# Two-block network on one core: who loads in the untaken overflow branch, and which engine subtracts at the start of the second block's mixers

## The chip, the cores and the metric

The kernel runs on one core of one Trainium2 chip. The metric is the device time of one execution in microseconds (us). Before the change three runs gave 1249.91, 1245.6 and 1245.42 us; their median is 1245.6.

## What is computed

The reference chains two blocks over 256 positions of 1024 channels, all in float32. The first block has two SwiGLU layers around two attention mixers, with 16 meta tokens ahead of the sequence. The second block has two layers, each of three mixers and a mixture of 32 experts:

```
def hybrid_layer(x, ...):
    hn = rms_norm(x, norm1_g)
    proj = jnp.einsum('bsd,df->bsf', hn, w_in)
    ya = mla_mixer(...)                 # low-rank attention, 8 heads
    yb = stick_breaking_mixer(...)      # 4 heads
    yc = pool_mixer(...)                # means over windows of 2, 4, 8, 16
    x = x + jnp.einsum('bsm,md->bsd', jnp.concatenate([ya, yb, yc], axis=-1), w_out)
    return x + hier_moe(rms_norm(x, norm2_g), w_group, b_group, w_expert, b_expert,
                        w_gate, w_up, w_down)

def second_block(x, ...):
    for l in range(2):
        x = hybrid_layer(x, ...)
    return rms_norm(x, final_g)
```

`rms_norm` multiplies each position by r = rsqrt(mean(x*x) + eps) and then by a gain for each channel. In `hier_moe` a position picks one of four groups of eight experts by the largest group probability, and in it the two likeliest experts.

## The kernel before

**Weights.** All weights are one array of units of 128 x 2048 float32 (1 MB, some shorter). `Stream.load` (L308) issues one unit as a DMA on SyncE's queue into a ring of eight raw buffers. `Stream.split` cuts a unit into two tiles of 1024 columns and makes of each a pair whl: a high part, by a ScalarE cast to fp32r (L326), and a low part, raw minus high, by a subtraction (L327). VectorE subtracts, or GpSimd while `st.spare` is set. There are four whl buffers. `take` hands a tile to the matmuls; `done` frees tiles and, unless `hold` is on, makes the next splits; `release` makes the splits that were held back. A product of two split operands is three matmuls (high x high, high x low, low x high). If the next unit belongs to the experts, which use raw units unsplit, `split` only counts it in `owed`, and `restart` makes these splits once the experts are through. A split has a higher priority in the scheduler, by 60 places, unless it is called with late=False.

**Order.** The program is written once; a scheduler orders each engine's instructions, by readiness and priority. Each engine then works through its own list. The DMAs of SyncE's queue use eight semaphores in turn, so at most eight loads are on their way.

**Block 2.** For each of two layers, called layer 1 and layer 2 here: `mixers2` (565 to 663 us and 899 to 1004 us of the trace), then `moe`. `mixers2` transposes x (xT), multiplies by the gain and splits into xnh (ScalarE) and xnl (VectorE) in eight steps of `gsplit`, and takes r by `rstd`: squares sq on ScalarE (L1134), their sum ss, and three short steps rs, rs, r on VectorE (L456 to L458). The products use x times gain without r; r is multiplied in afterwards. `m2_low_products` computes four products "low" of 24 matmuls each (t = 0 to 3, `wcol2`), one whl tile each. To multiply by r along the columns, r is spread: dg = ident * r on VectorE (L1214), rb = one x dg on TensorE, a copy to SBUF on VectorE (L1216); low * rb (L1225) then frees the PSUM banks that the next products, qk, are waiting for.

In layer 1 the first splits for the mixers come from the second SwiGLU layer of block 1, whose last act is the addition of its result py to x (L1084), four VectorE instructions.

**Experts.** `moe` works in eight batches b of four experts, 12 units each (eight for gate and up, gu; four for down, y). The raw ring is lent nine more buffers there, 17 in all. The result y of a batch is split into yh (ScalarE, L435) and yl (VectorE, L436) and added into a sum by the matmuls sc.

**Overflow.** An expert has 32 slots per batch. If more positions want one, `overflow` (L1721ff.) computes the rest in a second pass, behind batch 5. It reads a flag into a register on the engines (L1725, TENSOR_LOAD) and stands in a branch (L1728). With these inputs the flag is zero and the branch is not taken, but each engine has the branch's instructions in its list and jumps over them. In the branch SyncE loads weights into the buffers of yh and yl (L1740).

Of the kernel before, what the change touches and what calls it, by code (L numbers as in the profile page):

```python
# [12 lines left out]
OP = mybir.AluOpType  # L13
# [252 lines left out]
def run(*gens):  # L266
    for g in gens:
        for _ in g:
            pass


class Stream:
# [63 lines left out]
        for i in range(s.S):  # L336
            s.split(False)

    def restart(s):

        n, s.owed = s.owed, 0
        for i in range(n):
            s.split()

    def take(s, a=None):
        while s.used not in s.tiles:
# [38 lines left out]
class KB:  # L385
    R, S = 8, 4
    E = 5
    NW = 11

    def __init__(s, es, tc, a, out, dbg=None, stop=None):  # L390
        s.es, s.tc, s.nc, s.a, s.out, s.dbg, s.stop = es, tc, tc.nc, a, out, dbg or {}, stop
# [746 lines left out]
    def mixers2(s, l, p):  # L1138
        nc, st = s.nc, s.st
        v = s.v = {}  # L1140
# [10 lines left out]
        r = v["r"] = p.tile([128, 2], F32, name="r")  # L1151
# [3 lines left out]
            s.tr(pt[k][:, i * 128:i * 128 + 128], s.x[:, i, k * 128:k * 128 + 128])  # L1155
        for k in range(8):
            s.gsplit(xh[:, k, :], xl[:, k, :], pt[k][:, :T], g[:, k:k + 1])
        s.rstd(p, r)
        v["rb"] = p.tile([128, T], F32, name="rb")
        v["mix"] = p.tile([128, 2, 256], F32, name="mix")  # L1160
        v["ph"] = p.tile([128, 2, T], F32R, name="ph")
# [40 lines left out]
    def m2_low_products(s, p):  # L1202
        st, v = s.st, s.v
        q = [s.ps("low") for t in range(4)]
        for t in range(4):
            run(s.wcol2(q[t][:, :T]))
            if t == 1:
                st.spare = True
                st.release()
                st.spare = False  # L1210
                rb = s.ps("rb", tag="y")
                for i in range(2):
                    dg = s.w(p, "dg")
                    s.nc.vector.tensor_scalar(dg[:, :128], s.ident, v["r"][:, i:i + 1], None, op0=OP.mult)  # L1214
                    s.mm(rb[:, i * 128:i * 128 + 128], s.one, dg[:, :128], i == 0, True)
                s.nc.vector.tensor_copy(v["rb"], rb[:, :T])  # L1216
        return q

# [412 lines left out]
    def experts(s, l, p, px, OH, OHT, comb):  # L1631
        nc, st = s.nc, s.st
        v = nc.vector
# [4 lines left out]
        n = 0  # L1638
# [39 lines left out]
        for b in range(NB):  # L1678
# [3 lines left out]
            for k in range(8):  # L1682
                w = unit()
# [28 lines left out]
        s.exp_set()  # L1712
        down(NB - 1, hT)
        es.close()
        st.spare = True
        st.restart()
        st.spare = False
        if l:
            s.final()

    def overflow(s, l, p):

        nc, a = s.nc, s.a
        v = nc.vector
        some = nc.values_load(s.flag[0:1, 0:1], min_val=0, max_val=1)  # L1725
        gain = s.g("n2")[:, 8 * l:8 * l + 8]
        units = a["weights"][s.moe_base[l]:s.moe_base[l] + 12 * NB].rearrange("(b n) p (e f) -> b n p e f", b=NB, e=4)
        with s.tc.If(some > 0):  # L1728
            with s.phase(f"ov{l}") as po:

                W = po.tile([128, 2, 32], F32, name="oW")
                v.tensor_scalar(W, s.place, float(SL), None, op0=OP.is_gt)
                v.tensor_mul(W, W, s.r.to_broadcast([128, 2, 32]))
                W4 = W.rearrange("p i (g e) -> p i g e", g=4)
                for i in range(2):
                    v.tensor_mul(W4[:, i], W4[:, i], s.ci[:, i, None, 0:8].to_broadcast([128, 4, 8]))

                def load(b, n, j):
                    w = p.tile([128, 512], F32, name="yh" if n % 2 else "yl")
                    nc.sync.dma_start(w, units[b, n, :, j, :])  # L1740
                    return w

                XT = p.tile([128, 8, 128], F32, name="XT", bufs=3)
                for i in range(2):
                    for k in range(8):
                        q = s.ps("ogat")
                        s.tr(q[:, :128], s.x[:, i, k * 128:k * 128 + 128])
                        nc.scalar.activation(XT[:, k, :], q[:, :128], AF.Copy, scale=gain[:, k:k + 1])
                    for e in range(32):
                        b, j = divmod(e, 4)  # L1750
                        q = s.ps("ogu")
                        for k in range(8):
                            s.mm(q, XT[:, k, :], load(b, k, j), k == 0, k == 7)
                        sg = po.tile([128, 256], F32, name="osg")
                        nc.scalar.activation(sg, q[:, :256], AF.Silu, scale=s.r[:, i])
                        hid = po.tile([128, 256], F32, name="ohid")
                        v.scalar_tensor_tensor(hid, q[:, 256:], W[:, i, e:e + 1], sg, op0=OP.mult, op1=OP.mult)
                        q = s.ps("ohT")
                        for f in range(2):
                            s.tr(q[:, f * 128:f * 128 + 128], hid[:, f * 128:f * 128 + 128])  # L1760
                        hT = po.tile([128, 256], F32, name="ohT")
                        nc.scalar.copy(hT, q[:, :256])
                        for c in range(2):
                            q = s.ps("oy")
                            for f in range(2):
                                s.mm(q, hT[:, f * 128:f * 128 + 128], load(b, 8 + 2 * c + f, j), f == 0, f == 1)
                            xs = s.x[:, i, c * 512:c * 512 + 512]
                            v.tensor_add(xs, q, xs)
# [49 lines left out]
```

## Time and profile before

| what | us |
|---|---|
| median of three runs | 1245.6 |
| profiled execution | 1246.45 |
| its span in the trace | 1244.7 |
| TensorE busy | 1110.2 (89%) |
| VectorE busy | 560.6 (45%) |
| ScalarE busy | 464.1 (37%) |
| GpSimd busy | 146.0 (12%) |

In the rows below, PE is TensorE, DVE VectorE, ACT ScalarE, POOL GpSimd and SP SyncE; SPq is SyncE's queue. Times are us from the start of the span. A row of the timeline is start, busy us, engine, line, operation, names out<-in, shape, count, and in brackets the idle time of the engine just before, with the instruction whose end ended it. A high share of busy time is a mean over stages with different limits, so each stage is to be read by itself: by what its engines wait for and by how fast its loads run.

### The profile page before, as it was taken

The page shows a single profiled execution, that of the slowest core. Times are in us where ns is not written, and L with a number is a line of the kernel's source. Part 1 is how long each engine was busy: PE and PEld are TensorE (multiplying, and loading weights), DVE is VectorE, ACT ScalarE, POOL GpSimd, SP SyncE. Part 2 cuts the span into 40 slices and gives each one's busy share as a digit, 9 for nine tenths or more (in the row PEclk, how much of TensorE's full clock was granted, in tenths as well). Part 3 has the DMA queues.
Part 4 walks back from the last instruction along what each step waited for, and adds up shares of the span by engine and source line. Part 5 has one row for each costly group of instructions (what it writes and reads, how often), then busy time and mean ns, then how long its engine had stood idle before and what let it go on. Part 6 is the DMA issues. An engine that isn't in the chain of part 4 may idle for free. (4 is left out here: it accounts for less than half of the span.)

```text
span 1244.7 us, 18667 instructions
## 1 busy us (share of the span) xinstructions
PE 1110.2 (89%) x7530; PEld 840.1 (67%) x7530; DVE 560.6 (45%) x1081; ACT 464.1 (37%) x888; POOL 146.0 (12%) x151
## 2 busy tenths in 40 slices
PE   7999999999999999998998997863889989968545
PEld 7999999888799999997997532310289864313111
DVE  5555555679857555555755111100276452101002
ACT  6444444467545444445752010000257420000002
POOL 0222221000012212225110000000033000000001
PEclk9999999999999999998999899886989998988679
DMA  9754454643214545444427999999964299999986
GB/s 364 279 182 163 154 191 175 159 182 125 80 69 172 200 172 200 173 184 143 160 102 293 387 420 420 420 417 371 420 259 158 83 363 398 420 419 419 416 359 248
DMA packets 46470, 321.20 MB, mean 258 GB/s; under 512 B 5560, under 2 KB 5688, under 8 KB 8992
## 3 DMA queue, kind: packets, MB, share of 16 engines
q1 hardware_dynamic: 44640, 314.96, 64.8%
q0 software_dynamic: 1264, 4.26, 1.6%
q8 instruction: 64, 1.05, 0.3%
q10 hardware_dynamic: 464, 0.63, 0.1%
q14 instruction: 38, 0.31, 0.1%
HBM read 317.13 MB, written 2.69 MB: 257 GB/s over the span
## 5 line engine op out<-in xcount | busy, mean ns | idle before, releaser
L326 ACT CAST whl<-raw 128x1024 fp32r<-128x1024 f32 (+1 forms) x213 | 221.1, 1040 | 258.8 <-PE pu L410 53.1
L327 DVE TENSOR_TENSOR whl<-raw,whl 128x1024 fp32r<-128x1024 f32 (+1 forms) x203 | 249.8, 1232 | 147.1 <-ACT whl L326 147.0
L410 PE MATMUL gu<-raw,XT 128*32 128x512 f32 x1024 | 141.1, 651 | 33.4 <-DMA raw<-in_weights_dram 15.7
L410 PE MATMUL pg<-xh,whl 128*128 128x272 f32 (+1 forms) x704 | 137.4, 287 | 1.0 <-DVE gt L616 1.0
L410 PE MATMUL pu<-xh,whl 128*128 128x272 f32 (+1 forms) x704 | 136.2, 284 | 0.0
L410 PEld LDWEIGHTS pg<-xh,whl 128*128 128x128 f32 x704 | 113.2, 190 | 2.2 <-issue 1.1
L410 PEld LDWEIGHTS pu<-xh,whl 128*128 128x128 f32 x704 | 112.3, 188 | 0.0
L410 PEld LDWEIGHTS gu<-raw,XT 128*32 128x32 f32 x1024 | 28.4, 115 | 108.1 <-issue 72.6
L410 PE MATMUL pg<-xl,whl 128*128 128x272 f32 (+1 forms) x352 | 100.7, 286 | 0.0
L410 PE MATMUL y<-raw,hT 128*32 128x512 f32 x512 | 84.4, 679 | 18.2 <-DMA raw<-in_weights_dram 18.2
L410 PE MATMUL pu<-xl,whl 128*128 128x272 f32 (+1 forms) x352 | 100.3, 285 | 0.0
L436 DVE TENSOR_TENSOR yl<-y,yh 128x512 fp32r<-128x512 f32 x32 | 22.1, 691 | 144.6 <-ACT yh L435 144.6
L1699 DVE SCALAR_TENSOR_TENSOR hid<-gu,comb,sg 128x256 f32<-128x256 f32 x16 | 7.7, 484 | 152.7 <-ACT sg L1697 152.7
L436 POOL TENSOR_TENSOR hl<-hid,hh 128x272 fp32r<-128x272 f32 (+1 forms) x44 | 57.7, 1312 | 123.7 <-ACT hh L435 123.7
L435 ACT CAST yh<-y 128x512 fp32r<-128x512 f32 x32 | 18.8, 586 | 142.4 <-PE y L410 104.7
L410 PEld LDWEIGHTS pg<-xl,whl 128*128 128x128 f32 x352 | 66.9, 190 | 0.8
L410 PE MATMUL sc<-yh,OHT 128*128 128x512 f32 x64 | 25.8, 487 | 45.9 <-ACT yh L435 45.9
L410 PE MATMUL pd<-hh,whl 128*128 128x272 f32 x352 | 66.7, 289 | 0.0
L410 PE MATMUL gat<-OH,x 128*128 128x256 f32 x256 | 63.9, 401 | 3.0 <-DVE OH L1582 3.0
L410 PEld LDWEIGHTS pu<-xl,whl 128*128 128x128 f32 x352 | 66.2, 188 | 0.0
L410 PEld LDWEIGHTS sc<-yh,OHT 128*128 128x128 f32 x64 | 10.5, 207 | 78.4 <-ACT yh L435 77.5
L410 PEld LDWEIGHTS gat<-OH,x 128*128 128x128 f32 x256 | 48.8, 198 | 21.4 <-issue 11.7
(410 smaller groups left out, 2038.7 us busy)
## 6 DMA issues: line engine op xcount, KB each, us to landing
raw<-in_weights_dram SPq DMA_DIRECT2D x292, 1024.0 KB, 14.2
raw<-in_weights_dram SPq DMA_DIRECT2D x4, 768.0 KB, 4.2
raw<-in_weights_dram SPq DMA_DIRECT2D x5, 512.0 KB, 7.5
dl<-line POOLq DMA_DIRECT2D x1, 1600.0 KB, 36.9
tb<-dl POOLq DMA_DIRECT2D x1, 1088.0 KB, 6.4
x<-in_x_dram SPq DMA_DIRECT2D x4, 256.0 KB, 5.0
c<-in_consts_dram POOLq DMA_DIRECT2D x1, 954.0 KB, 6.5
sm<-in_smalls_dram SPq DMA_DIRECT2D x1, 712.0 KB, 18.6
```

What stands on the lines that cost most here:

```text
L326: s.kb.nc.scalar.copy(h[:, :n], raw)
L327: (s.kb.nc.gpsimd if s.spare is True or s.spare and j else s.kb.nc.vector).tensor_sub(l[:, :n], raw, h[:, :n].bitcast(F32))
L410: s.nc.tensor.matmul(out, l, r, start=start, stop=stop, skip_group_check=True)
L435: s.nc.scalar.copy(h, x)
L436: (s.nc.gpsimd if gpsimd else s.nc.vector).tensor_sub(l, x, h.bitcast(F32))
L1699: v.scalar_tensor_tensor(hid, q[:, 256:], comb[:, b, 0:1], sg, op0=OP.mult, op1=OP.mult)
```

## The change

Five edits, all in block 2.

1. `overflow`: the flag is read on four engines only, without SyncE, and without the check of its bounds. The loads in the branch are issued by GpSimd.
2. `restart(n)` makes up to n of the owed splits, without the raised priority. It is called in `mixers2` after the fourth `gsplit` (one split), after the last (two), and after `rstd` (the rest), and no longer at the end of `moe`, where GpSimd did the subtractions.
3. The `release` in `m2_low_products` at t = 1 does its subtractions on VectorE.
4. dg is computed behind t = 0.
5. rb and its copy move from t = 1 to t = 2.

```
-    def restart(s):
-        n, s.owed = s.owed, 0
+    def restart(s, n):
+        n = min(n, s.owed)
+        s.owed -= n
         for i in range(n):
-            s.split()
+            s.split(False)
...
+    OV = (mybir.EngineType.PE, mybir.EngineType.Activation, mybir.EngineType.DVE, mybir.EngineType.Pool)
...
             s.gsplit(xh[:, k, :], xl[:, k, :], pt[k][:, :T], g[:, k:k + 1])
+            if k == 3:
+                st.restart(1)
+        st.restart(2)
         s.rstd(p, r)
+        st.restart(st.S)
...
             run(s.wcol2(q[t][:, :T]))
+            if t == 0:
+                dg = [s.w(p, "dg") for i in range(2)]
+                for i in range(2):
+                    s.nc.vector.tensor_scalar(dg[i][:, :128], s.ident, v["r"][:, i:i + 1], None, op0=OP.mult)
             if t == 1:
-                st.spare = True
                 st.release()
-                st.spare = False
+            if t == 2:
                 rb = s.ps("rb", tag="y")
                 for i in range(2):
-                    dg = s.w(p, "dg")
-                    s.nc.vector.tensor_scalar(dg[:, :128], s.ident, v["r"][:, i:i + 1], None, op0=OP.mult)
-                    s.mm(rb[:, i * 128:i * 128 + 128], s.one, dg[:, :128], i == 0, True)
+                    s.mm(rb[:, i * 128:i * 128 + 128], s.one, dg[i][:, :128], i == 0, True)
                 s.nc.vector.tensor_copy(v["rb"], rb[:, :T])
...
         es.close()
-        st.spare = True
-        st.restart()
-        st.spare = False
...
-        some = nc.values_load(s.flag[0:1, 0:1], min_val=0, max_val=1)
+        some = nc.values_load(s.flag[0:1, 0:1], engines=s.OV, min_val=0, max_val=1, skip_runtime_bounds_check_because="the flag is the result of a comparison")
...
-                    nc.sync.dma_start(w, units[b, n, :, j, :])
+                    nc.gpsimd.dma_start(w, units[b, n, :, j, :])
```

SyncE's list before, from the last loads of the first branch to the second check. The second of the two jumps behind the branch waits for all eight semaphores of SyncE's DMAs.

```order
L1740 DMA yh<-in_weights_dram 128x512
L1728 UNCONDITIONAL_BRANCH x2
L1725 ISA x2
L308 DMA raw<-in_weights_dram 128x2048 x18
L308 DMA raw<-in_weights_dram 128x1024
L308 DMA raw<-in_weights_dram 128x2048 x89
L1725 TENSOR_LOAD flag
L1728 COMPARE_AND_BRANCH
```

The same stretch of SyncE's list after.

```order
L308 DMA raw<-in_weights_dram 128x1024
L308 DMA raw<-in_weights_dram 128x2048 x74
L1732 UNCONDITIONAL_BRANCH
L308 DMA raw<-in_weights_dram 128x2048 x33
L308 DMA raw<-in_weights_dram 128x1024
L308 DMA raw<-in_weights_dram 128x2048 x74
L1732 UNCONDITIONAL_BRANCH
L308 DMA raw<-in_weights_dram 128x2048 x26
```

Of the check a plain jump without a semaphore is left on SyncE; the flag, the conditional branch, the branch's loads and the two ISA instructions, which add to the eight semaphores, have gone from its list. The first yh and yl behind the check wait for the semaphores of the queue that holds the branch's loads: SyncE's before, GpSimd's after.

VectorE before, at the start of layer 1's mixers (ss, rs, rs and r are the steps to 1/rms).

```order
L620 TENSOR_TENSOR hid<-pu,rT 128x256
L1084 SCALAR_TENSOR_TENSOR x<-py,x 128x512 x4
L441 SCALAR_TENSOR_TENSOR xnl<-xT,sm,xnh 128x256 x8
L1135 TENSOR_TENSOR ss<-ss 128x2
L456 SCALAR_TENSOR_TENSOR rs_6247<-ss,rs_6246 128x2
L457 SCALAR_TENSOR_TENSOR rs_6247<-rs_6247,rs_6246 128x2
L458 SCALAR_TENSOR_TENSOR r<-rs_6247,rs_6246 128x2
L1214 TENSOR_SCALAR dg<-ident,r 128x128 x2
L1216 COPY rb<-rb 128x256
```

VectorE after, at the same place.

```order
L622 TENSOR_TENSOR hid<-pu,rT 128x256
L327 TENSOR_TENSOR whl<-raw,whl 128x1024
L1086 SCALAR_TENSOR_TENSOR x<-py,x 128x512 x4
L327 TENSOR_TENSOR whl<-raw,whl 128x1024
L443 SCALAR_TENSOR_TENSOR xnl<-xT,sm,xnh 128x256 x8
L1137 TENSOR_TENSOR ss<-ss 128x2
L327 TENSOR_TENSOR whl<-raw,whl 128x1024
L458 SCALAR_TENSOR_TENSOR rs_6247<-ss,rs_6246 128x2
L459 SCALAR_TENSOR_TENSOR rs_6247<-rs_6247,rs_6246 128x2
L460 SCALAR_TENSOR_TENSOR r<-rs_6247,rs_6246 128x2
L1216 TENSOR_SCALAR dg<-ident,r 128x128 x2
L327 TENSOR_TENSOR whl<-raw,whl 128x1024
```

Four subtractions that stood in GpSimd's list now stand among these: one ahead of the additions to x, one ahead of xnl, one ahead of rs and one behind dg.

VectorE after, at the start of layer 2's mixers; before, xnl stands there as one row of eight, and no subtraction ahead of dg.

```order
L1673 TENSOR_TENSOR x<-sc,x 128x512 x2
L443 SCALAR_TENSOR_TENSOR xnl<-xT,sm,xnh 128x256 x4
L327 TENSOR_TENSOR whl<-raw,whl 128x1024
L443 SCALAR_TENSOR_TENSOR xnl<-xT,sm,xnh 128x256 x4
L327 TENSOR_TENSOR whl<-raw,whl 128x1024 x2
L1137 TENSOR_TENSOR ss<-ss 128x2
L327 TENSOR_TENSOR whl<-raw,whl 128x1024 x2
L458 SCALAR_TENSOR_TENSOR rs_11737<-ss,rs_11736 128x2
L327 TENSOR_TENSOR whl<-raw,whl 128x1024
L459 SCALAR_TENSOR_TENSOR rs_11737<-rs_11737,rs_11736 128x2
L460 SCALAR_TENSOR_TENSOR r<-rs_11737,rs_11736 128x2
```

Six subtractions stand ahead of r there. On TensorE rb stands behind 72 of the 96 matmuls of low in layer 1 (55 before) and behind 79 in layer 2 (48 before).

## Rows read from the trace of the kernel before

**Rows 1.** The page, 40 equal slices: TensorE busy, granted clock (tenths), GB/s.

```profile
PE   7999999999999999998998997863889989968545
PEclk9999999999999999998999899886989998988679
GB/s 364 279 182 163 154 191 175 159 182 125 80 69 172 200 172 200 173 184 143 160 102 293 387 420 420 420 417 371 420 259 158 83 363 398 420 419 419 416 359 248
```

**Rows 2.** Windows of 5 us: busy per engine, granted clock, DMA share, GB/s.

```profile
860.00:865.00 5.00, 1.94 (x6) 0.70 (x10) 0.69 (x1) 0.59 (x1) 0.00 (x0) 0.50 0.43 129
...
1195.00:1200.00 5.00, 0.71 (x2) 0.50 (x2) 0.69 (x1) 0.59 (x1) 0.00 (x0) 0.50 0.23 93
1200.00:1205.00 5.00, 5.00 (x20) 0.91 (x18) 0.00 (x0) 0.00 (x0) 0.00 (x0) 0.50 0.96 359
```

**Rows 3.** Timeline of ScalarE at the two checks.

```profile
862.43 0.59 ACT L435 CAST yh<-y 128x512 fp32r<-128x512 f32 x1 [20.86 <-SPq L1728]
...
1198.66 0.59 ACT L435 CAST yh<-y 128x512 fp32r<-128x512 f32 x1 [16.80 <-SPq L1728]
```

**Rows 4.** Waits of SyncE's queue, 840 to 920 us: total, times, longest.

```profile
SPq L1728 <- SPq L1728: 18.9, 7, 5.1
```

**Rows 5.** Timeline of TensorE around the checks.

```profile
863.06 1.22 PE L410 MATMUL sc<-yh,OHT 128*128 128x512 f32 x2 [13.55 <-ACT yh L435]
...
1171.52 3.42 PE L410 MATMUL gu<-raw,XT 128*32 128x512 f32 x16 [11.40 <-issue]
...
1183.52 1.02 PE L410 MATMUL y<-raw,hT 128*32 128x512 f32 x2 [0.49 <-DMA raw<-in_weights_dram]
```

**Rows 6.** Timeline of TensorE, start of layer 1's mixers.

```profile
567.44 0.38 PE L410 MATMUL low<-xnh,whl 128*128 128x256 f32 x1 [0.16 <-DVE xnl L441]
...
578.31 1.19 PE L410 MATMUL rb<-dg,one 128*128 128x128 f32 x4 [4.12 <-DVE dg L1214]
...
586.27 0.28 PE L410 MATMUL qk<-xnh,whl 128*128 128x256 f32 x1
```

**Rows 7.** Timeline of VectorE, start of layer 1's mixers.

```profile
563.98 2.48 DVE L1084 SCALAR_TENSOR_TENSOR x<-py,x 128x512 f32<-128x512 f32 x4 [4.19 <-PE py L410]
566.90 3.23 DVE L441 SCALAR_TENSOR_TENSOR xnl<-xT,sm,xnh 128x256 fp32r<-128x256 f32 x8 [0.44 <-ACT xnh L440]
...
575.31 2.27 DVE L457 SCALAR_TENSOR_TENSOR rs<-rs,rs 128x2 f32<-128x2 f32 x1
577.61 0.16 DVE L458 SCALAR_TENSOR_TENSOR r<-rs,rs 128x2 f32<-128x2 f32 x1
```

**Rows 8.** Timeline of GpSimd in both layers of block 2.

```profile
562.59 4.73 POOL L327 TENSOR_TENSOR whl<-raw,whl 128x1024 fp32r<-128x1024 f32 x2
...
572.88 4.67 POOL L327 TENSOR_TENSOR whl<-raw,whl 128x1024 fp32r<-128x1024 f32 x2 [2.16 <-ACT whl L326]
...
695.89 0.67 POOL L1144 TENSOR_TENSOR wr<-sm 128x288 f32<-128x288 f32 x1 [67.38 <-PE ohT L418]
...
904.36 9.37 POOL L327 TENSOR_TENSOR whl<-raw,whl 128x1024 fp32r<-128x1024 f32 x4 [207.70 <-ACT whl L326]
```

**Rows 9.** Window of 4 us behind rb in layer 1, columns as in Rows 2.

```profile
578.00:582.00 4.00, 3.69 (x17) 3.73 (x18) 1.54 (x5) 0.75 (x2) 0.73 (x1) 0.50 0.72 262
```

**Rows 10.** Timeline of TensorE, start of layer 2's mixers.

```profile
904.33 0.58 PE L410 MATMUL low<-xnh,whl 128*128 128x256 f32 x1 [4.59 <-ACT whl L326]
...
906.76 0.79 PE L410 MATMUL low<-xnh,whl 128*128 128x256 f32 x2 [1.63 <-POOL whl L327]
...
920.76 0.28 PE L410 MATMUL qk<-xnh,whl 128*128 128x256 f32 x1
```

**Rows 11.** The page's costliest groups: busy, mean ns of one, idle before.

```profile
L327 DVE TENSOR_TENSOR whl<-raw,whl 128x1024 fp32r<-128x1024 f32 (+1 forms) x203 | 249.8, 1232 | 147.1 <-ACT whl L326 147.0
```

**Rows 12.** Timeline of ScalarE, start of layer 2's mixers.

```profile
897.86 3.04 ACT L440 ACTIVATE xnh<-xT,sm 128x256 fp32r<-128x256 f32 x8 [1.55 <-PE sc L410]
```

**Rows 13.** The chain of waits, its shares of the span by line.

```profile
by line: DMA raw<-in_weights_dram 1.5%; PE y L410 0.5%; PE sc L410 0.5%; ACT sq L1778 0.2%; ACT yh L435 0.2%; DVE x L1666 0.1%; DVE raw L1792 0.1%; issue 0.1%; DVEq L1814 0.1%; DVE rs L457 0.0%; DVE rs L458 0.0%; ACT rs L448 0.0%; DVE rs L4
```

## Prediction

> **What bounds the kernel now.** I began with the page's slices [rows 1]. In the two expert stages (slices 23 to 29 and 34 to 39) the loads run at 417 to 420 GB/s, with one dip in each, 371 in slice 28 and 359 in slice 39, where TensorE is busy only 3 and 4 tenths. Outside the dips these stages last as long as their loads. In the mixers ahead of them (slices 19 to 21 and 30 to 32) TensorE is busy 8 tenths and more and the loads run far below what they reach later: there TensorE's chain is the bound. So a microsecond saved at the start of a mixer stage, or in a dip, should reach the end: what follows is TensorE's chain, and then a stream of loads whose buffers come free when the mixers are done.
>
> Next the windows of 5 us at the dips [rows 2]. In the first, 129 GB/s; against 418, the level of the stage, that is 5 x (1 - 129/418) = 3.5 us without loads. At the second, 93 and then 359 GB/s: 5 x (1 - 93/418) + 5 x (1 - 359/418) = 3.9 + 0.7 = 4.6 us.
>
> Then who waits there. ScalarE's first cast yh behind the overflow's check comes after 20.86 us of idle time in layer 1 and 16.80 in layer 2, and the releaser is SyncE's branch at L1728 [rows 3]; SyncE's queue waits at its own L1728, 18.9 us in all around the first dip [rows 4]. I read this so: SyncE gets past the branch not taken only when all its loads in flight have landed, and issues nothing meanwhile, so that the loads run dry. TensorE waits for that yh, 13.55 us in layer 1; in layer 2 it had been waiting for a load at 1183.52, just ahead of its own wait for yh [rows 5].
>
> Last the mixers' starts. In layer 1 TensorE runs 55 of the 96 matmuls of the low products from 567.44 on and then waits 4.12 us for dg up to 578.31, so from 574.19, because rb stands there [rows 6]. dg is late because r is: its second last step took 2.27 us on VectorE, the last one, of the same shape, 0.16 [rows 7]. GpSimd's two subtractions from 572.88 to 577.55 lie over the slow one and not over the fast one [rows 8]. Behind the wait TensorE's granted clock is 0.50, its 1.2 GHz level [rows 9]. In layer 2 TensorE waits 4.59 us for a cast and 1.63 more for GpSimd's first subtraction [rows 10]; GpSimd's four take 9.37/4 = 2.34 us each [rows 8], VectorE's 1.23 on average [rows 11].
>
> **The change, part by part.**
>
> 1. The check in layer 1. SyncE's branch has no wait any more, so its loads go on: 3.5 us. This holds if TensorE doesn't keep the buffers instead. Its own jump over the overflow's code stays (11.40 us in layer 2), but TensorE had made that good by 1183.52 [rows 5]. Bounds: 2 (part of the gap comes back, since each load still waits for a buffer) to 4.5 (the gap of layer 2).
>
> 2. The check in layer 2, in the same way: 4.6 us. Bounds 2.5 to 6; the upper end is for TensorE's pile of work at half clock behind the wait, whose only sign in the loads is the 0.7 us above, taken three times.
>
> 3. The mixers of layer 1. The subtractions leave GpSimd, so r is early, and rb stands 17 matmuls later: no wait for dg. At the pace of the first 55 (6.75/55, about 0.12 us each) 96 matmuls take 11.5 us, with rb's 0.6 12.1; they took from 567.44 to 586.27, where qk starts, 18.8 [rows 6]. So 6.7 us can go, 4.1 of wait and 2.6 of half clock. But VectorE's first subtraction now stands ahead of the residual additions. GpSimd still runs one from 562.59 to 564.97 [rows 8]; VectorE's would end about 1.1 behind it (an estimate, a little under its mean of 1.23), at 566.05, and the additions, now from 563.98 [rows 7], start 2.1 later. The second subtraction, 1.23 less the gap of 0.44 that stood ahead of xnl [rows 7], adds 0.8. The low products begin 2.9 later, at 570.3, and end at 582.4: 3.9 us gained. Bounds: 1.5 (TensorE's clock falls in the longer wait ahead of them; a product of 24 matmuls at 0.21 us, about their pace in layer 2 behind 906.76, instead of 0.12 costs 2.2) to 6.7 (the subtractions delay nothing).
>
> The 2.1 us rest on the row of 2.27 [rows 7]: a VectorE instruction on operands in SBUF ends when GpSimd's does. The Trainium skill, "SBUF — State Buffer", section "Who interferes with whom", has this as a rule: when a VectorE instruction with two SBUF inputs and a GpSimd one that reads SBUF meet, the later to start is blocked to the end of the other. By it the term is 3.9, and the trace agrees (2.27 against 0.16); without it the subtraction would end 1.23 behind its cast and the term would be 5.2.
>
> 4. The mixers of layer 2. All subtractions go to VectorE and the casts move up among the gain products. The first cast now stands behind the eight xnh, which begin at 897.86 and take 3.04 [rows 12], and the squares, and ends just ahead of 904.33 [rows 10]; behind the fourth xnh it starts at about 899.4 and ends at 900.4, and the subtraction ends near 901.7, against TensorE's starts at 904.33 and 906.76 [rows 10]. The first product still at half clock, 24 x 0.21 = 5.1, ends at 906.8; at 0.12 the second ends at 909.7, the third at 912.6. r's chain stands behind the sixth tile's subtraction, which waits for the second product: 909.7 + 1.05 + 1.23 = 912.0, then two steps and dg, 0.9 together: 912.9. rb stands 79 matmuls in, at 913.4, so TensorE hardly waits; qk starts at 916.1 instead of 920.76: 4.6 us. Bounds 2.5 (r two microseconds later) to 6.
>
> GpSimd's queue now holds the loads of the overflow that aren't run. It comes to the check early: L1144, the first thing behind the check in its queue, ran at 695.89 [rows 8], 150 us before anyone needs the check.
>
> **Sum:** 3.5 + 4.6 + 3.9 + 4.6 = 16.6 us. The profiled execution took 1246.45 (span 1244.7 and 1.75 around it), 0.85 above the median of 1245.6. So 1229.85 for it, and **1229.0** at the median.
>
> **The rivals.**
>
> A. The forecast, 1229.0.
>
> B. The subtractions cost VectorE's path what they cost GpSimd's: layer 1 gains 1.5, layer 2 one. For: r's chain stands behind two more subtractions, and the additions behind one. Against: each takes half of GpSimd's time. 1245.6 - 8.1 - 2.5 = 1235.0.
>
> C. The last batch runs at half clock. Now TensorE has work piled up behind the wait and keeps its clock at 9 tenths in slice 40; without the pile it works from load to load to the end. In the chain of waits its y and sc have 0.5% each [rows 13], 12.4 us of 1244.7 together; less some 3 ahead of the last load that the chain goes through, 9.4, and twice that at half clock: 1229.0 + 9.4 = 1238.4. Against: in the other expert slices, where it works from load to load, the clock is mostly 8 or 9 tenths [rows 1].
>
> D. Both delays of parts 3 and 4 are hidden: 6.7 + 5.5 + 3.5 + 5 = 20.7, 1224.9.
>
> E. Slower: GpSimd behind the check. VectorE and ScalarE now wait, at their first yl and yh, for semaphores that GpSimd sets behind its jump over some 780 rows. In layer 1 yh is due when TensorE's y is done, 863.06 less the 13.55 of wait: 849.5. The free buffers (17 less the eight on their way, at 2.5 us for a load of 1 MB) cover about 22 us of lateness; from there on each microsecond counts in full, in each layer. 40 us late would give 1245.6 - 8.5 + 2 x 18 = 1273.1. Against: GpSimd passes 150 us earlier, and TensorE's jump over as much code took 11.40 us. The Trainium skill, "Runtime: NRT & Kernel Launch", section "Instruction fetch mechanics", says that a taken branch out of the fetched window waits for its target to be fetched; it gives no price, and by TensorE's row GpSimd is still early.
>
> F. The change doesn't do what it says, and the loads still run dry. The order shows no wait at SyncE's branch. Only 8.5 us of the mixers: 1237.1.
>
> **How the numbers follow.** Chances: A 0.55, B 0.18, C 0.08, D 0.13, E 0.02, F 0.04. Half a per cent, 6.2 us, is about what a measurement of this kernel can tell from no change; faster is below 1239.4. A and D lie there whole, B and F nearly, C for the most part: 0.91; same 0.06, slower 0.03. The lower bounds sum to 8.5, the upper to 23.2: 1237.1 and 1222.4. All at one end is unlikely; C lies just outside. The range 1221.5 to 1238 leaves out E and the outer parts of B, C and F.
>
> **What would show it.** Right: no window under 400 GB/s at the two checks and no wait of ScalarE on the branch; in layer 1 no wait of TensorE ahead of rb, and from the first low product to qk about 12 us instead of 18.8; in layer 2 the first low product 2 to 3 us earlier behind the last sc, and qk 4 to 5. Wrong: low products of layer 1 over 3 us later, or at half clock (B); granted clock 0.50 behind the last load (C); ScalarE or VectorE released by GpSimd at the check (E); loads still running dry there (F).

## The result, and the profile after

The changed kernel takes 1232.51 us (median of four runs, 1226.56 to 1236.81), the kernel before 1246.42 (four runs, 1245.42 to 1249.91): ratio 0.9878, interval 0.9838 to 0.9917, wholly below 1. The forecast was 1229.0 in a range of 1221.5 to 1238. The profiled execution, 1236.81 us with a span of 1235.0, is the slowest of the four.

The page of the changed kernel, slices as in [rows 1]:

```profile
PE   7999999999999999999999998767799989978565
PEclk9999999999889999999999899778899988988687
GB/s 365 277 185 169 154 175 192 145 184 120 103 35 161 181 185 190 180 196 156 193 77 229 390 421 420 420 419 418 421 345 145 86 331 399 420 420 420 416 418 241
```

Both dips in the loads are gone: 416 to 421 from slice 24 to 29 and from 35 to 39. But PEclk has two 8s in slices 11 and 12, in the first block, where [rows 1] has 9s and where the change has no instruction. The windows of 10 us there, first of the changed kernel (busy time of PE, PEld, DVE, ACT, POOL; granted clock; DMA share; GB/s):

```profile
330.00:340.00 10.00, 10.00 (x36) 6.66 (x36) 5.37 (x23) 3.88 (x14) 0.00 (x0) 0.64 0.00 1
340.00:350.00 10.00, 10.00 (x44) 7.68 (x44) 5.43 (x22) 3.48 (x12) 0.00 (x0) 0.68 0.00 1
```

and of the kernel before:

```profile
330.00:340.00 10.00, 10.00 (x55) 7.16 (x56) 8.02 (x36) 5.64 (x21) 0.00 (x0) 1.00 0.00 1
340.00:350.00 10.00, 10.00 (x67) 8.53 (x66) 6.82 (x23) 5.07 (x17) 0.00 (x0) 1.00 0.01 2
```

In 20 us the changed kernel does 80 matmuls where the other does 122, and the first block ends 6.3 us later. A difference of 10 us in the spans thus hides one of 16 behind it. So I compare stages, each from one matmul's start to another's. The third column is a second profile of the same changed kernel.

| stage, us | before | after | after, again | forecast gain |
|---|---|---|---|---|
| to the last py (first block) | 564.5 | 570.8 | 566.7 | 0 |
| last py to first gu (mixers, layer 1) | 121.7 | 117.1 | 117.4 | 3.9 |
| first gu to last sc (experts, layer 1) | 211.3 | 208.2 | 207.8 | 3.5 |
| last sc to first gu (mixers, layer 2) | 123.5 | 119.4 | 120.3 | 4.6 |
| first gu to the last load's landing | 210.6 | 206.9 | 205.7 | 4.6 |
| last landing to the end | 13.1 | 12.6 | 12.7 | 0 |
| span | 1244.7 | 1235.0 | 1230.6 | 16.6 |

Without the first block the two profiles give 15.9 and 16.3 us, against the forecast's 16.6.

At the checks ScalarE's first yh is released by TensorE's y, 4.1 and 1.2 us after the work before it; before, it was released by SyncE's branch, after 20.86 and 16.80 [rows 3]. Timeline of ScalarE after:

```profile
848.40 0.59 ACT L437 CAST yh<-y 128x512 fp32r<-128x512 f32 x1 [4.09 <-PE y L412]
...
1179.16 0.59 ACT L437 CAST yh<-y 128x512 fp32r<-128x512 f32 x1 [1.24 <-PE y L412]
```

SyncE's queue waited 18.9 us at the branch around the first check [rows 4]. After, it has no wait at its jump there; what it waits for most, from 830 to 920 us, is an earlier load (total, times, longest):

```profile
SPq L308 <- DMA raw<-in_weights_dram: 55.4, 26, 3.0
```

Start of layer 1's mixers after: TensorE,

```profile
573.00 2.56 PE L420 MATMUL xT<-ident,x 128*128 128x128 f32 x16 [1.86 <-DVE x L1086]
576.32 0.38 PE L412 MATMUL low<-xnh,whl 128*128 128x256 f32 x1 [0.76 <-DVE xnl L443]
584.90 0.61 PE L412 MATMUL rb<-dg,one 128*128 128x128 f32 x4
588.17 0.28 PE L412 MATMUL qk<-xnh,whl 128*128 128x256 f32 x1
```

VectorE,

```profile
569.81 2.53 DVE L327 TENSOR_TENSOR whl<-raw,whl 128x1024 fp32r<-128x1024 f32 x1 [3.75 <-ACT whl L326]
572.26 2.47 DVE L1086 SCALAR_TENSOR_TENSOR x<-py,x 128x512 f32<-128x512 f32 x4
...
582.50 0.16 DVE L459 SCALAR_TENSOR_TENSOR rs<-rs,rs 128x2 f32<-128x2 f32 x1
```

and GpSimd.

```profile
568.86 2.40 POOL L327 TENSOR_TENSOR whl<-raw,whl 128x1024 fp32r<-128x1024 f32 x1
...
708.51 0.67 POOL L1146 TENSOR_TENSOR wr<-sm 128x288 f32<-128x288 f32 x1 [78.12 <-remote]
```

All times here are 6.3 later than in [rows 6 to 8] by the first block. The price that the prediction named is there: VectorE's subtraction begins at 569.81 under GpSimd's, which ends at 571.26, and ends 1.08 later; it takes 2.53 instead of 1.23, the additions start 2.0 late (572.26 less 6.27 is 565.99 against 563.98), and TensorE waits 1.86 for them ahead of xT. The step rs that took 2.27 [rows 7] takes 0.16, TensorE has no wait at rb, and from the first low product to qk there are 11.85 us instead of 18.83.

Start of layer 2's mixers after, TensorE:

```profile
899.04 0.39 PE L412 MATMUL low<-xnh,whl 128*128 128x256 f32 x1 [0.68 <-ACT whl L326]
900.30 0.50 PE L412 MATMUL low<-xnh,whl 128*128 128x256 f32 x2 [0.76 <-DVE whl L327]
910.14 0.68 PE L412 MATMUL rb<-dg,one 128*128 128x128 f32 x4 [0.35 <-DVE dg L1216]
912.70 0.28 PE L412 MATMUL qk<-xnh,whl 128*128 128x256 f32 x1
```

The waits of 4.59 and 1.63 [rows 10] have become 0.68 and 0.76, and r's chain is just not quite in time (0.35).

### The profile page after: what moved, and what is told of

Read it like the earlier page. It is cut to its first block, busy times and chain, and to the rows that moved or that the text cites. A ratio compares the mean times of both kernels' runs of the same rounds, so it can differ in the third digit from the quotient of the medians.

```text
span 1235.0 us, 18659 instructions
## 1 busy us (share of the span) xinstructions
PE 1117.6 (90%) x7530; PEld 839.4 (68%) x7530; DVE 559.5 (45%) x1089; ACT 464.1 (38%) x888; POOL 127.9 (10%) x143
## 4 chain that ended last, share of the span: by engine, by line
PE 66%; DMA 26%; DVE 4%; ACT 2%; issue 1%; SPq 0%; DVEq 0%; ACTq 0%
DMA raw<-in_weights_dram 26%; PE pg L412 10%; PE pu L412 10%; PE wo L412 5%; PE pd L412 5%; PE py L412 5%; PE gat L412 3%; PE gu L412 3%; PE sc L412 2%; PE po L412 2%; PE qk L412 2%; PE z L412 1%; PE low L412 1%; DVE whl L327 1%; PE qb L412 1%; PE vs L412 1%
## 5 line engine op out<-in xcount | busy, mean ns | idle before, releaser
L327 DVE TENSOR_TENSOR whl<-raw,whl 128x1024 fp32r<-128x1024 f32 (+1 forms) x211 | 260.9, 1238 | 152.0 <-ACT whl L326 150.9
L412 PE MATMUL gu<-raw,XT 128*32 128x512 f32 x1024 | 146.5, 679 | 47.0 <-DMA raw<-in_weights_dram 28.7
L412 PE MATMUL y<-raw,hT 128*32 128x512 f32 x512 | 78.0, 695 | 18.1 <-DMA raw<-in_weights_dram 16.7
L1704 ACT ACTIVATE sg<-gu,comb 128x256 f32<-128x256 f32 x16 | 7.6, 474 | 178.6 <-PE gu L412 178.6
L412 PEld LDWEIGHTS y<-raw,hT 128*32 128x32 f32 x512 | 13.8, 117 | 66.1 <-issue 27.3
```

The source lines that it names most:

```text
L327: (s.kb.nc.gpsimd if s.spare is True or s.spare and j else s.kb.nc.vector).tensor_sub(l[:, :n], raw, h[:, :n].bitcast(F32))
L412: s.nc.tensor.matmul(out, l, r, start=start, stop=stop, skip_group_check=True)
L1704: nc.scalar.activation(sg, q[:, :256], AF.Silu, scale=comb[:, b, 1:2])
```

## The experiments

**The same kernel again.** No edit.

> The changed kernel, unaltered, once more. Its profiled run lost 6.3 us between 330 and 350 us, in the first block, where the granted clock was 0.64 and 0.68 and the change has no instruction. Theory 1 (chance in the clock): the drop comes and goes; a new profile shows it elsewhere or not at all, without it the run ends 6 us earlier, and the time against the kernel before is 15 to 18 us less, ratio about 0.987. Theory 2 (the change itself brings the drop, by another order of work or another load pattern): the new profile shows 0.6 to 0.7 at 330 to 350 us again, and runs under 1230 us stay rare.

1232.61 us (1231.75 to 1233.43, five runs), ratio 0.9867 (0.9841 to 0.9893). The runs of the kernel before in this series, and in the next three experiments, have a median of 1250.89 (1246.35 to 1252.57), above its 1246.42 of the first series; between the kernels of the series their medians can be compared directly. The clock is at 1.00 from 330 to 350 us, and falls elsewhere in the first block:

```profile
230.00:240.00 10.00, 9.47 (x53) 8.11 (x52) 3.69 (x6) 3.64 (x7) 0.00 (x0) 0.83 0.64 105
```

This is theory 1: the drop comes and goes and moves. In the other twelve profiles of this document the first block takes 564.3 to 567.4 us. But only the profiled span became shorter, by 4.4 us; the median is that of the first series, so the one drop does not set it. Theory 2's second sign, few runs under 1230, is there too in this series, so a weak tie to the kernel isn't excluded.

**The check alone.** The kernel before with the following, and with `OV` as in the change:

```
-        some = nc.values_load(s.flag[0:1, 0:1], min_val=0, max_val=1)
+        some = nc.values_load(s.flag[0:1, 0:1], engines=s.OV, min_val=0, max_val=1, skip_runtime_bounds_check_because=...)
...
-                    nc.sync.dma_start(w, units[b, n, :, j, :])
+                    nc.gpsimd.dma_start(w, units[b, n, :, j, :])
```

> The kernel before with the first edit alone (the flag read without SyncE, the branch's loads on GpSimd). Forecast: both gaps in the loads go, layer 1's expert stage is 3.3 us shorter, layer 2's 4 to 5, in all 8 us: ratio 0.9935. The mixers keep their waits: TensorE 4.1 us ahead of rb in layer 1, 4.6 and 1.6 us at the start of layer 2. Rival (the gaps are hidden by TensorE's chain, and the mixers bring everything): under 3 us, ratio over 0.9975.

1237.64 us, ratio 0.9905 (0.9875 to 0.9935). By stages, layer 1's experts take 207.95 instead of 211.27 and layer 2's 206.51 instead of 210.64, together 7.5 us less, near the 8 expected. The mixers are as before (first low to qk 18.44 and 16.25). The rival falls: the gaps weren't hidden. The medians of whole runs differ by 13.3 us, more than the stages account for; where the rest lies no profile shows.

**The mixers alone.** The changed kernel with those two lines back as they were.

> The changed kernel with the first edit undone: the check and its loads stay with SyncE. Forecast from the profile after: layer 1's mixers 4.4 us shorter, layer 2's start 6.6, in all 11 us, ratio 0.991; both gaps in the loads are there again, ScalarE's yh released by SyncE's branch after some 17 to 21 us. Rival (the check's and the mixers' gains aren't additive, since an earlier start of the loads meets a longer drain): under 8 us.

1239.39 us, ratio 0.9918 (0.9888 to 0.9949), 6.8 above the changed kernel in the same series. The gaps are there again (windows of 5 us, columns as above, first and second check):

```profile
855.00:860.00 5.00, 0.01 (x1) 0.01 (x1) 0.03 (x1) 0.59 (x1) 0.00 (x0) 0.50 0.50 208
860.00:865.00 5.00, 5.00 (x16) 1.40 (x20) 0.66 (x1) 0.00 (x0) 0.00 (x0) 0.50 0.79 300
...
1190.00:1195.00 5.00, 1.52 (x6) 0.70 (x10) 0.69 (x1) 0.59 (x1) 0.00 (x0) 0.50 0.30 66
```

with the same cause, as ScalarE's timeline and the waits of SyncE's queue show:

```profile
859.35 0.59 ACT L437 CAST yh<-y 128x512 fp32r<-128x512 f32 x1 [20.87 <-SPq L1732]
```

```profile
SPq L1732 <- SPq L1732: 18.9, 7, 5.3
```

The expert stages take 211.71 and 209.84, 3.9 and 4.2 more than in the second profile after. The mixers keep 3.6 and 3.4 us of their gain by stages. By stages the parts nearly add, as the forecast assumed: the two half kernels, each with its own gain, give 7.5 + 7.0 = 14.5, and the same four stages of the whole change 15.4 and 16.0. The 7.0 is less than the 11 expected and under the rival's 8, but not for the rival's reason: the wait at the branch is as long as before (20.87 against 20.86). The 11 took the gain at the start of layer 2 for that of the whole stage, and the step from gat to gu behind it gives back 2.1 (below). The medians don't show that the parts add: 13.3 and 11.5 against 18.3 for the whole. The kernel before stands in all three of these differences, and its nine runs spread over 6.2 us, so additivity rests on one profile of each kernel.

**SyncE in the check, but without loads there.** In the changed kernel only

```
-        some = nc.values_load(s.flag[0:1, 0:1], engines=s.OV, min_val=0, max_val=1, skip_runtime_bounds_check_because=...)
+        some = nc.values_load(s.flag[0:1, 0:1], min_val=0, max_val=1)
```

> The changed kernel, but all five engines read the flag and check its bounds, SyncE too; the branch's loads stay on GpSimd. Question: is it SyncE's part in the check that drains the loads, or the loads in its branch? Theory 1 (SyncE has to settle the semaphores of the loads that stand in its branch, and these count the weights' loads too): without loads there it waits for nothing, no window of 5 us under 400 GB/s at either check, expert stages as after (208 and 206 to 207 us). Theory 2 (the branch itself drains SyncE's queue): the gaps are back, both stages 3 to 5 us longer.

1233.82 us (one run). No gap at either check, and SyncE's queue doesn't wait at the branch; the windows at the first check:

```profile
850.00:855.00 5.00, 4.52 (x29) 1.32 (x22) 0.69 (x1) 0.59 (x1) 0.00 (x0) 1.00 1.01 421
855.00:860.00 5.00, 4.00 (x26) 0.81 (x26) 0.00 (x0) 0.37 (x1) 0.00 (x0) 1.00 1.01 419
860.00:865.00 5.00, 2.21 (x16) 0.36 (x16) 0.00 (x0) 0.00 (x0) 0.00 (x0) 0.84 1.02 423
```

So it isn't the branch on SyncE that drains the loads, it is that loads of SyncE's own queue stand in it. Layer 2's experts take 204.97 us. Layer 1's take 209.55, 1.7 more than in the second profile after. That loss doesn't lie at the check, where no window is under 416 GB/s. At the stage's start the loads run at 338, 377 and 415 GB/s from 680 to 710 us, against 374, 392 and 386; this explains little of it, and its cause is open.

**dg and rb back at t = 1.** The changed kernel with

```
-            if t == 0:
-                dg = [s.w(p, "dg") for i in range(2)]
...
-            if t == 2:
                 rb = s.ps("rb", tag="y")
                 for i in range(2):
+                    dg = s.w(p, "dg")
...
```

> The changed kernel with dg and rb put back to t = 1. Subtractions as in the changed kernel. In layer 1 rb stands 55 matmuls in, and dg is ready at about that time (in the profile after 11.1 us behind the first low product's start, the 55 matmuls take 6.7): a wait of 4 us is expected if dg's time doesn't move. In layer 2 rb stands 48 in, about 6 us behind the start, and dg comes 11 us behind it: a wait of 4 to 5 us. Theory 1 (the later place of rb is worth 4 us in each layer and the subtractions' engine is not): low to qk 16 us or more in both. Theory 2 (the subtractions on VectorE make r early enough by themselves): under 13 us in layer 1.

1231.39 us (one run). TensorE in layer 1:

```profile
570.20 0.58 PE L412 MATMUL low<-xnh,whl 128*128 128x256 f32 x1
577.57 0.68 PE L412 MATMUL rb<-dg,one 128*128 128x128 f32 x4 [0.45 <-ACT whl L326]
582.86 0.28 PE L412 MATMUL qk<-xnh,whl 128*128 128x256 f32 x1
```

TensorE waits 0.45 us ahead of rb, and from low to qk it takes 12.66 us instead of 11.86, so theory 2 holds. The 4 us that I expected rested on a wrong number: 11.1 us is dg's time in layer 2; in layer 1 dg is ready 7.1 us behind the first low product (583.44 against 576.32), and 55 matmuls take 6.7. In layer 2 the test is void: the scheduler put rb behind 79 matmuls as in the changed kernel, wherever the program has it.

**Layer 1's release back on GpSimd.** The changed kernel with

```
             if t == 1:
+                st.spare = True
                 st.release()
+                st.spare = False
```

> The changed kernel with the four subtractions of the release at t = 1 in layer 1 back on GpSimd; rb stays at t = 2. Nothing then stands ahead of the additions on VectorE, so the first low product is 2.6 us earlier (2.96 us behind the last py's start instead of 5.57); but GpSimd's subtractions lie over r's steps again, and dg is ready 10.9 us behind the first low matmul as before the change, where 72 matmuls take 8.7. Theory 1: TensorE waits 2 us at rb, low to qk 14 us instead of 11.9, in all about even with the changed kernel: moving these subtractions to VectorE was worth nothing once rb stood later. Theory 2 (VectorE's share is what made the 4.4 us): layer 1's mixers 3 us longer.

1229.94 us (one run). TensorE:

```profile
567.21 0.39 PE L412 MATMUL low<-xnh,whl 128*128 128x256 f32 x1 [0.16 <-DVE xnl L443]
578.13 0.68 PE L412 MATMUL rb<-dg,one 128*128 128x128 f32 x4 [2.17 <-DVE dg L1216]
```

and VectorE:

```profile
573.03 2.05 DVE L458 SCALAR_TENSOR_TENSOR rs<-ss,rs 128x2 f32<-128x2 f32 x1 [1.20 <-ACT rs L451]
575.11 2.29 DVE L459 SCALAR_TENSOR_TENSOR rs<-rs,rs 128x2 f32<-128x2 f32 x1
```

This is theory 1, closely: 14.27 us from low to qk, with the start 2.6 earlier, so 17.23 from the last py to qk against 17.43 in the changed kernel. Now the last two experiments together. Before, that stretch took 21.79; the later rb alone brings 4.6, the other engine alone 3.6 (12.66 + 5.57 = 18.23), and both together 4.4. They cure the same wait, and each is nearly enough.

**Two of the four on GpSimd.** The changed kernel with

```
             if t == 1:
+                st.spare = True
+                st.some(2)
+                st.spare = False
                 st.release()
```

where `some(n)` makes the first n of the held splits.

> The changed kernel, but of the four subtractions that the release at t = 1 makes in layer 1 the first two go to GpSimd and two stay on VectorE. Nothing then stands ahead of the additions to x on VectorE. Theory 1 (VectorE's first subtraction is blocked behind GpSimd's and delays the additions by 2.1 us, the second delays xnl by 0.8): the low products start 2.9 us earlier, qk too, and dg is still early, so 2.5 to 3 us less than the changed kernel. Theory 2 (the delay is hidden, or r becomes late since GpSimd's subtractions lie over it again): the start of the low products moves, but TensorE waits for dg ahead of rb by as much, and nothing is gained.

1227.31 us (1226.02 to 1228.84), ratio 0.9821 (0.9796 to 0.9847), 5.3 below the changed kernel in the same series. TensorE and VectorE:

```profile
567.92 0.38 PE L418 MATMUL low<-xnh,whl 128*128 128x256 f32 x1 [0.16 <-DVE xnl L449]
576.58 0.68 PE L418 MATMUL rb<-dg,one 128*128 128x128 f32 x4
```

```profile
564.46 2.48 DVE L1092 SCALAR_TENSOR_TENSOR x<-py,x 128x512 f32<-128x512 f32 x4 [4.19 <-PE py L418]
```

This is theory 1: the additions start at once, the low products 2.96 us behind the last py instead of 5.57, and r is still early. From the last py to the first gu the kernel takes some 2.5 us less (114.78 against 117.13 and 117.35). Of the rest of the 5.3 the profiles show 1.8 in the first block, which the edit doesn't touch, and the other stages are 0.7 longer than in the second profile after; what else lies in the medians has no profile.

**Layer 2's restart on GpSimd, at the new place.** `st.spare` is set around the three calls of `restart`.

> The changed kernel, layer 2's restarted splits at their new, early place but with the subtractions on GpSimd. Theory 1 (the earlier place gives the gain, the engine little): first low as after, 3.0 us behind the last sc, and low to qk under 15.5 us. Theory 2 (2.34 us for a subtraction instead of 1.23, and r's steps blocked behind them): TensorE waits a microsecond more for the first tile and 2 to 4 for dg, low to qk 16 to 18.

1230.61 us (one run). The first matmul comes as early, the second waits for GpSimd as long as before the change [rows 10]:

```profile
892.82 0.58 PE L412 MATMUL low<-xnh,whl 128*128 128x256 f32 x1 [0.24 <-ACT whl L326]
895.26 0.79 PE L412 MATMUL low<-xnh,whl 128*128 128x256 f32 x2 [1.65 <-POOL whl L327]
```

From low to qk it takes 16.88 us, against 13.65 and 14.61: theory 2 in size, 2 to 3 us, but only half by its mechanism. TensorE does wait a microsecond more for the first tile. It doesn't wait for dg, though, because the scheduler put rb behind 94 of the 96 matmuls here (79 in the changed kernel); instead qk waits 0.83 us for low * rb. Against the 14.61 these are 1.2 us, by which the second matmul comes later behind the first (2.44 instead of 1.26), and 0.8. So what the engine alone costs with rb in its old place is not shown. The place alone gives 3.9 us at the first matmul.

**The first cast ahead of the gain products.** On top of the kernel with two subtractions on GpSimd:

```
+        st.restart(1)
         for k in range(8):
             s.gsplit(xh[:, k, :], xl[:, k, :], pt[k][:, :T], g[:, k:k + 1])
             if k == 3:
                 st.restart(1)
-        st.restart(2)
+        st.restart(1)
```

Its base ran beside it once more.

> The changed kernel with two of layer 1's four subtractions on GpSimd, once more, as the base for the next kernel. The first time 5.3 us less than the changed kernel, of which its profile shows 2.5 in layer 1's mixers and 1.8 in the first block, where the changed kernel's clock fell for a while at 230 us and this one's didn't. Expected here: ratio 0.981 to 0.985 to the kernel before; the first block 564 to 565 us where its clock stays at 1.00.

> As the one beside it, and in layer 2 the first restarted split stands ahead of the gain products instead of behind the fourth. Theory 1 (TensorE waits for the first tile): the cast stands behind the first xnh, the first low product comes 1 us earlier behind the last sc (2 us instead of 3), TensorE's idle time gets shorter, its clock stays up in the low products, and qk comes 1 to 2 us earlier. Theory 2 (r's chain is the limit, TensorE waited 0.35 us for dg already): the low products start earlier and TensorE waits that much longer at rb; nothing gained.

Base 1230.87 us (1228.53 to 1233.49), ratio 0.9872 (0.9854 to 0.9890), outside what I expected: its profiled stages agree with the first time within 0.3 us, but two of its four runs took 1232.81 and 1233.49. They have no profile. The first block's drop cost 2.2 us in one profile and 6.3 in another, so it could be that, but this is not shown. With the first cast moved: 1225.24 us (1224.69 to 1226.04), ratio 0.9822 (0.9808 to 0.9835), the best of all here. The first low product comes 2.07 us behind the last sc instead of 2.99, low to qk takes 14.14 instead of 14.47: 1.3 us together, by theory 1. Another 1.7 lie in the step from gat to gu, which leads to the last experiment.

**1.45 us later.** From gat to gu, where TensorE gathers the experts' slots, most profiles with the changed mixers took 12.2 to 12.6 us in layer 2 (not the restart on GpSimd, 10.47, and the first cast ahead, 10.45), and those with the mixers unchanged 9.96 and 10.09, with the same matmuls. TensorE, before and then after:

```profile
1010.87 3.60 PE L410 MATMUL gat<-OH,x 128*128 128x256 f32 x8 [0.74 <-DVE OH L1582]
...
1015.58 5.45 PE L410 MATMUL gat<-OH,x 128*128 128x256 f32 x24 [0.74 <-DVE OH L1582]
```

```profile
1003.03 3.78 PE L412 MATMUL gat<-OH,x 128*128 128x256 f32 x8 [0.74 <-DVE OH L1589]
...
1008.24 7.32 PE L412 MATMUL gat<-OH,x 128*128 128x256 f32 x24 [0.74 <-DVE OH L1589]
```

The granted clock is 0.50 for most of these ten us after, for some 3.5 us before. Windows of 5 us, before and then after:

```profile
1010.00:1015.00 5.00, 4.09 (x14) 3.21 (x13) 3.30 (x18) 1.83 (x5) 0.00 (x0) 0.66 1.02 426
1015.00:1020.00 5.00, 4.42 (x21) 3.91 (x22) 3.10 (x8) 0.00 (x0) 0.00 (x0) 1.00 1.01 419
```

```profile
1005.00:1010.00 5.00, 4.26 (x13) 3.48 (x12) 2.11 (x7) 0.00 (x0) 0.00 (x0) 0.50 0.99 418
1010.00:1015.00 5.00, 5.00 (x20) 4.19 (x20) 2.20 (x6) 0.00 (x0) 0.00 (x0) 0.79 0.92 382
```

To move the moment and little else, the kernel with two subtractions on GpSimd computes half of layer 2's last low product twice (more is 4 there and 0 elsewhere):

```
         h, lo = s.st.take(8)
+        for k in range(more):
+            s.mm3(out, h[:, k, :], lo[:, k, :], s.xnh[:, k, :], s.xnl[:, k, :], k == 0, k == more - 1)
```

> The kernel with two subtractions on GpSimd, and in layer 2 twelve matmuls of the last low product are computed twice (the first pass is overwritten), which makes TensorE's mixers there 1.45 us longer. Question: with the changed mixers the step from the first gather of the experts' slots to the first gu takes 12.2 to 12.6 us in layer 2, where the granted clock stays at 0.50 for 9 us; in the kernels with the mixers unchanged, and in layer 1, 9.9 to 10.6 and 3.5 us. Theory 1 (it hangs on the moment at which TensorE gets there): 1.45 us later the step takes 10 to 10.6 us again, and the run is not longer than without the added work. Theory 2 (it hangs on the order of the work in that step, which the change altered): 12.2 again, and the run 1.5 us longer.

1232.21 us (one run; its first block is 2.4 us longer). In layer 2 the step takes 10.60 us, so theory 2 falls, and the added work is paid back: from the first low product to gu it takes 117.0 us, against 117.3 in its base. And layer 1, whose code is unaltered, now shows the long form, 12.68 against 10.08 and 10.17 in the two profiles of the base:

```profile
672.15 3.78 PE L418 MATMUL gat<-OH,x 128*128 128x256 f32 x8 [0.74 <-DVE OH L1601]
677.37 7.53 PE L418 MATMUL gat<-OH,x 128*128 128x256 f32 x24 [0.74 <-DVE OH L1601]
...
1001.23 3.78 PE L418 MATMUL gat<-OH,x 128*128 128x256 f32 x8 [0.74 <-DVE OH L1601]
1006.45 5.45 PE L418 MATMUL gat<-OH,x 128*128 128x256 f32 x24 [0.74 <-DVE OH L1601]
```

Theory 1 needs one correction: the moment is not the time since the start of the run. With the restart on GpSimd layer 1's first gat also starts at 672.14 us, and its step takes 10.59. What sorts all 26 steps of the 13 profiles is where the stretch at 0.50 begins, counted from the first gat, by the clock that the traces hold: from 0.4 us ahead of it to 0.6 behind it in the steps of 9.96 to 10.17 us, 0.8 to 1.8 ahead in those of 12.18 to 12.68, and 2.1 to 2.8 ahead in those of 10.45 to 10.60. Just ahead of it TensorE waits 1.58 and 0.74 us for VectorE, in the short form as in the long. What sets the beginning is open.

## Why the prediction was right, point by point

1. *The check in layer 1, 3.5 us.* It brought 3.1 and 3.5 us in the two profiles, 3.3 alone, and 3.9 were lost again when it was undone. The cause is confirmed and made narrower: it is the loads of SyncE's own queue inside the branch. TensorE's jump stayed (11.40 us of idle time before, 11.70 after, in layer 2) and stayed hidden, as said.

2. *The check in layer 2, 4.6.* It brought 3.7 and 5.0, 4.1 alone, and 4.2 were lost again when it was undone.

3. *Layer 1's mixers, 3.9.* They brought 4.5 and 4.3. The two numbers under the forecast were 2.1 and 0.8 us of delay and 12.1 for the products: measured were 2.0, 2.6 for both delays, and 11.86. The Trainium skill's rule that a VectorE instruction with two SBUF inputs and a GpSimd one that reads SBUF block each other, the later to the end of the earlier ("SBUF — State Buffer", "Who interferes with whom") was the right one of the two I weighed: the subtraction took 2.53 us instead of 1.23. The kernel that takes the subtraction away from there got some 2.5 us back. What was not right is the account: I put the gain on the subtractions leaving GpSimd together with the later rb, and nearly all of it comes with either alone.

4. *Layer 2's mixers, 4.6.* They brought 4.1 and 3.2, by two errors that offset one another, so that the term came this near is luck. First, I let the first product run at half clock throughout (5.1 us), as before the change. TensorE's granted clock was 1.00 over the whole of it in the first profile after, and 0.66 over one window of 5 us in the second:

```profile
895.00:900.00 5.00, 4.24 (x22) 4.04 (x23) 4.96 (x7) 5.00 (x13) 0.00 (x0) 0.66 1.01 421
```

TensorE's waits had become shorter, but they are alike in these two profiles (0.68 and 0.76 us against 0.67 and 0.76), so they don't explain the clock by themselves. From the last sc to qk the gain is 6.7 and 5.7. Second, the gather behind the mixers then loses 2.4 and 2.2, which I didn't foresee: I assumed that a stage which starts earlier keeps its length. The sign "2 to 3 us earlier" for the first low product was not what the working says (900.4 against 904.33, 3.9); 3.9 is what came.

5. *The rivals.* B (VectorE's subtractions cost as much as GpSimd's) did not come; the nearest to it is 0.35 us at rb. C (half clock in the last batch) shows in part: the last windows of loads run at 0.50 to 0.65, but TensorE is through the rest at 1.00, and from the last landing to the end it takes 12.6 instead of 13.1. D (delays hidden) is excluded in layer 1 by the 1.86 us; in layer 2 the gain up to qk does reach D's 5.5, and the gather takes it back. E (GpSimd late at the check) did not come, but its jump is dear. Its L1146 ran at 708.51, and 695.89 [rows 8] plus the 1.9 us by which the stage starts later is 697.8: 10.7 us later, with 140 us to spare. In the eleven profiles with the branch's loads on GpSimd this instruction starts 25.0 to 31.4 us behind the first gat, in the two with them on SyncE 19.9 and 20.4, so it is these loads that cost GpSimd the 5 to 11 us. F (the loads still run dry) is excluded.

6. *The sum.* 16.6 us were forecast. The stages give 15.9 and 16.3, the medians of the first series 13.9 and those of the second 18.3, in which the runs before took longer. What the forecast left out is the first block: its clock, where the change has no instruction, made one profile of the changed kernel 6.3 us longer, more than any term of the sum. Whether it also spreads the runs that have no profile isn't shown. One reading was loose, and the sum doesn't use it: at the start of the expert stages, in slices 23 and 34, [rows 1] has 387 and 398 GB/s and not 417 to 420.

## What to carry to other kernels

In this kernel a branch that is never taken still cost its engine what stands in it: with loads in it, all that the queue had on the way had to land first, and the cure was to give the loads to an engine whose queue was idle. Of two cures for one wait try each alone, since together they may bring no more than one, and the one that also moves work ahead of the critical chain can be dropped; here two subtractions given back to GpSimd were worth some 2.5 us. And before a change of one per cent is read from whole runs, compare the stages: one drop of the clock elsewhere can be larger than any part of the effect.

## What the runs showed of the hardware

The step from gat to gu, the same matmuls behind the same waits of 0.74 us, takes 10 to 12.7 us depending on where around its first gat the granted clock falls to 0.50, and 1.45 us of added work ahead of it made it 1.6 shorter. What decides where the clock falls I can't say from these runs.

The blocking between VectorE and GpSimd works both ways. In layer 2 a small sum of GpSimd, 0.74 us at 918.08 before, takes 1.46 after, where it begins under a subtraction of VectorE (913.98, 1.23 us):

```profile
914.34 1.46 POOL L1235 TENSOR_TENSOR sq<-sq 128x256 f32<-128x256 f32 x1 [205.07 <-ACT sq L1234]
```
